# A masked softmax whose GpSimd set-up becomes the first turn of its load loop

## The chip, the cores and the metric

The kernel runs on one core of a Trainium2 chip. The metric is the time of one execution on the device in microseconds (us), as the median of several runs; lower is better. The core has four compute engines that matter here, each with its own stream of instructions: VectorE (DVE), ScalarE (ACT), GpSimd (POOL) and TensorE (PE). SyncE (SP) only issues transfers. Sixteen DMA engines move data between the device memory and the on-chip memory. Transfers issued by SP go through one queue, those issued by POOL through another, and both are served by the same sixteen engines. The profile calls SP's queue q1, POOL's queue q0, and the queue that brings the engines their code q14.

## The reference

For each of 16 batches, a softmax over the first `length` columns of each row, and zero behind them:

```python
def setup_inputs():
    batch, heads, seq_q, seq_k = 16, 8, 256, 256
    return {
        "x": np.random.randn(batch, heads, seq_q, seq_k).astype(np.float32),
        "lengths": np.random.randint(seq_k // 2, seq_k, size=batch).astype(np.int32),
    }

def reference(x, lengths):
    result = np.zeros_like(x)
    for b in range(batch):
        length = lengths[b]
        masked = x[b, :, :, :length].copy()
        masked = masked - np.max(masked, axis=-1, keepdims=True)
        exp_masked = np.exp(masked)
        result[b, :, :, :length] = exp_masked / np.sum(exp_masked, axis=-1, keepdims=True)
    return result.astype(np.float32)
```

The draw is the same each time. A batch is 2048 rows of 256 columns in float32, 2 MB.

## The kernel before

**Tiles.** A batch lies on chip as 128 partitions x 16 rows x 256 columns, in one of eight slots of the tile `xt`; batch b is in slot b % 8. The work is done in place: a slot is loaded, clipped, exponentiated, divided and stored.

**Loads.** SP loads batches 0 to 3 whole, without waiting (L128 to L132). POOL loads batches 4 to 15 in a loop of six turns (L177), two batches in a turn (`par` 0 and 1). Of these batches only as many columns are loaded as are needed: `pick` (L147) is a tree of compares of the batch's length with the widths 160, 168, ... 240, and each of its twelve leaves holds one transfer of a fixed width (256 in the last). The tree stands twice in the loop, once for each `par`. Before its tree, each `par` reads the length into a register (L120 called from L180) and, from the second turn on, waits until its own load before has landed (L182, `s_sw`) and until the store that frees the slot is done (L183, `s_st`).

**Set-up on POOL.** Ahead of the loop POOL makes `iota_i` (L164), `ones` and `ones_c` (L167, L168), two small writes that raise the store semaphores once so that the loop's counts fit (L170), waits for two steps of DVE (L171), clears the columns from 160 on in slots 4 to 7 with four memsets (L173), and waits for the lengths, for its own memsets and for the load of batch 2 (L174 to L176). Columns behind a narrow load must hold something finite; from the ninth batch on a slot holds old results there.

**DVE.** From `iota_i` it makes `down` (L204), a large negative ramp; from the lengths, spread to all partitions by a PE matmul with `ones` (L189), it makes `len_s` (L212). Per batch it clips x by the minimum with `down` + `len_s` (L221), so that columns behind the length become hugely negative and their exponential is zero. When ACT is done with half a batch, DVE takes the reciprocal of the sums (L245) and multiplies (L248).

**ACT.** A loop over the 32 halves of batches (L321) runs eight exponentials with row sums each (L326).

**Stores.** SP, in order of batches, in one to three parts (L136 to L143). It begins when the third half has been exponentiated (L134). From batch 2 on it waits at the first part until the store two batches earlier is done (L140).

**End.** DVE checks the extremes of the row sums (L274 on); only if they are out of range a slower version with the true maximum runs, which doesn't happen with this draw. SP waits for all stores (L355).

Of the kernel before, what the change touches and what calls it, by code (L numbers as in the profile page):

```python
# [17 lines left out]
POOL = mybir.EngineType.Pool  # L18
# [3 lines left out]
def kernel(  # L22
# [6 lines left out]
    nc = tc.nc  # L29
    P = nc.NUM_PARTITIONS  # L30

    batch, heads, seq_q, seq_k = x.shape
# [8 lines left out]

    slots = 8
    ahead = 4
    assert slots - ahead == 4 and batch % slots == 0

    widths = list(range(160, 248, 8))
    low = widths[0]
# [18 lines left out]
    xt = pool.tile([P, slots, nt, seq_k], F32, name="xt")  # L66
    word64 = pool.tile([1, batch], mybir.dt.int64, name="word64")
    word = word64.bitcast(I32)
    len_b = pool.tile([1, batch], BF16, name="len_b")
    ones = pool.tile([1, P], BF16, name="ones")  # L70
    len_f = psum.tile([P, batch], F32, name="len_f")
    len_s = pool.tile([P, batch], F32, name="len_s")
    iota_i = pool.tile([P, seq_k], I32, name="iota_i")
# [4 lines left out]
    seed = pool.tile([1, 2], F32, name="seed")  # L78

    sum_low, sum_high = 1.0e-15, 1.0e30  # L80
    ones_c = pool.tile([P, 1], BF16, name="ones_c")
# [10 lines left out]
    s_st = [sem("s_st0"), sem("s_st1")]  # L92
    with tc.tile_critical(no_gpsimd_drain=True):  # L93
        s_word = sem("s_word")
        s_ones = sem("s_ones")
        s_lenb = sem("s_lenb")
        s_lenf = sem("s_lenf")
        s_ld = [sem(f"s_ld{k}") for k in range(ahead + 1)]

        s_sw = [sem("s_sw0"), sem("s_sw1")]  # L100

        s_iota = sem("s_iota")
        s_fill = sem("s_fill")
        s_v = sem("s_v")
# [13 lines left out]
        def length(engine, at):  # L118

            return nc.values_load(  # L120
                at,
                engines=[engine],
                skip_runtime_bounds_check_because="compared with constants, never an address",
            )
# [22 lines left out]
        def pick(v, n, slot, par, ws):  # L147

            if len(ws) == 1:
                w = ws[0]  # L150
                nc.gpsimd.dma_start(  # L151
                    out=xt[:, slot, :, :w], in_=x_n[:, n, :, :w]
                ).then_inc(s_sw[par], 16)
                return
            m = (len(ws) - 1) // 2
            with nc.gpsimd.If(v <= ws[m]):  # L156
                pick(v, n, slot, par, ws[: m + 1])
            with nc.gpsimd.Else():
                pick(v, n, slot, par, ws[m + 1 :])
# [1 line left out]
        x_n = x_f.rearrange("b p t c -> p b t c")  # L161
        x_g = x_f.rearrange("b p t c -> p b (t c)")
        o_g = out_f.rearrange("b p t c -> p b (t c)")
        nc.gpsimd.iota(  # L164
            iota_i, pattern=[[1, seq_k]], base=0, channel_multiplier=0
        ).then_inc(s_iota, 1)
        nc.gpsimd.memset(ones, 1.0).then_inc(s_ones, 1)  # L167
        nc.gpsimd.memset(ones_c, 1.0).then_inc(s_ones, 1)  # L168
        for par in range(2):
            nc.gpsimd.memset(seed[:, par : par + 1], 0.0).then_inc(s_st[par], 64)  # L170
        nc.gpsimd.wait_ge(s_v, 2)  # L171
        for b in range(ahead, slots):
            nc.gpsimd.memset(xt[:, b, :, low:], 0.0).then_inc(s_fill, 1)  # L173
        nc.gpsimd.wait_ge(s_word, 16)  # L174
        nc.gpsimd.wait_ge(s_fill, slots - ahead)
        nc.gpsimd.wait_ge(s_ld[ahead - 1], 16)  # L176
        with nc.Fori(0, (batch - ahead) // 2, 1, engines=[POOL]) as q:  # L177
            for par in range(2):
                n = 2 * q + (ahead + par)
                v_len = length(POOL, word[0:1, bass.ds(2 * n, 1)])  # L180
                with nc.gpsimd.If(q >= 1):  # L181
                    nc.gpsimd.wait_ge(s_sw[par], 16 * q)  # L182
                    nc.gpsimd.wait_ge(s_st[par], 64 * q)  # L183
                pick(v_len, bass.ds(n, 1), bass.ds(n % slots, 1), par, widths + [seq_k])


        nc.tensor.wait_ge(s_ones, 2)
# [198 lines left out]
```

## Time and profile before

| what | value |
|---|---|
| time, median of 3 runs | 156.16 us (155.8 to 156.35) |
| time of the profiled execution | 156.34 us |
| span of that execution in the profile | 154.7 us |
| DVE busy | 116.6 us, 75% of the span |
| ACT busy | 105.2 us, 68% |
| POOL busy | 19.0 us, 12% |
| bytes moved by the DMA engines | 62.09 MB, mean 401 GB/s |
| share of q1 (SP), q0 (POOL) in 16 engines' span | 65.7%, 32.1% |
| POOL's 12 issues of loads (L151) | mean 1064 ns each |
| POOL's 4 clearing memsets (L173) | mean 1391 ns each |

The span runs from the first to the last instruction of the program; the time has what lies around it as well. The profile names a group of work by its line, engine and operation, then the tile that it writes and those that it reads ("xt<-in_x_dram" is a load of x into `xt`). An engine's name with a q (POOLq, SPq) stands for its sequencer: reading registers, branching, waiting, issuing. In the chain of waits, "issue" is time for which the profile shows no cause.

### The profile page before, as it was taken

What the parts mean: (1) busy time and instruction counts of PE and PEld (TensorE: products, weight loads), DVE (VectorE), ACT (ScalarE), POOL (GpSimd) and SP (SyncE); (2) the same over time, 40 slices, a digit from 0 to 9 for tenths busy, and PEclk for the clock granted to TensorE, in tenths of its full rate; (3) what the DMA queues carried; (4) which work ended last, traced back from release to release, by engine and by line L of the source; (5) the groups of instructions that cost most, each with busy time, mean ns of one, the idle gap of its engine ahead of it and who ended that gap; (6) DMA issues with size and microseconds to landing.
All of it is one profiled execution on the core that took longest, in us unless ns stands there. A gap on an engine that the chain in (4) does not pass through costs nothing.

```text
span 154.7 us, 1341 instructions
## 1 busy us (share of the span) xinstructions
PE 0.3 (0%) x2; PEld 0.2 (0%) x2; DVE 116.6 (75%) x89; ACT 105.2 (68%) x514; POOL 19.0 (12%) x26
## 2 busy tenths in 40 slices
PE   0000000000000000000000000000000000000000
PEld 0000000000000000000000000000000000000000
DVE  1349999953999696979879696969669619696820
ACT  3097799992692959688695959595964914959300
POOL 4910031000220200202020020202001000000000
DMA  3999999999999999999999999999999999999991
GB/s 114 430 447 419 441 373 420 403 407 447 406 403 391 410 410 417 412 416 412 404 422 409 415 412 409 421 414 412 415 424 415 416 437 432 422 447 424 424 426 76
DMA packets 9989, 62.09 MB, mean 401 GB/s; under 512 B 850, under 2 KB 946, under 8 KB 6274
## 3 DMA queue, kind: packets, MB, share of 16 engines
q1 hardware_dynamic: 5904, 41.95, 65.7%
q0 software_dynamic: 4080, 20.12, 32.1%
q14 instruction: 3, 0.02, 0.0%
q10 hardware_dynamic: 2, 0.00, 0.0%
HBM read 28.51 MB, written 33.55 MB: 401 GB/s over the span
## 4 chain that ended last, share of the span: by engine, by line
DMA 77%; issue 7%; DVE 4%; ACT 3%; POOLq 3%; SPq 1%; ACTq 0%; POOL 0%; PE 0%; DVEq 0%
DMA xt<-in_x_dram 77%; ACT xt L326 3%; DVE xt L221 2%; DVE xt L248 1%; POOLq L120 1%; POOLq L156 1%; POOLq L151 1%; SPq L130 1%; DVE ends L274 0%; ACTq L326 0%; POOL xt L151 0%; SPq L132 0%; POOLq L181 0%; DVE bad L277 0%; DVE inv_sum L245 0%
## 5 line engine op out<-in xcount | busy, mean ns | idle before, releaser
L326 ACT ACTIVATE xt<-xt x256 | 102.4, 402 | 37.7 <-DVE xt L221 37.7
L248 DVE TENSOR_TENSOR xt<-xt,inv_sum 128x2048 f32<-128x2048 f32 x32 | 73.3, 2291 | 1.1
L326 ACT ACTIVATION_READ_ACCUMULATOR xt<-xt x256 | 48.0, 188 | 0.0
L221 DVE SCALAR_TENSOR_TENSOR xt<-down,len_s,xt 128x2048 f32<-128x2048 f32 (+1 forms) x17 | 37.8, 2221 | 13.6 <-DMA xt<-in_x_dram 13.5
L151 POOL DMA_DIRECT2D xt<-in_x_dram x12 | 12.8, 1064 | 96.0 <-DMA out_dram<-xt 54.2
L245 DVE RECIPROCAL inv_sum<-row_sum 128x8 f32<-128x8 f32 x32 | 6.3, 198 | 14.4 <-ACT xt L326 14.4
L173 POOL MEMSET xt<- 128x1536 f32 x4 | 5.3, 1391 | 1.1 <-DVE len_s L212 1.1
L318 ACT ACT_TABLE_LOAD x1 | 1.3, 1283 | 1.6 <-SPq L93 1.6
L204 DVE TENSOR_SCALAR down<-iota_i 128x256 f32<-128x256 int32 x1 | 0.3, 301 | 1.6 <-POOL iota_i L164 1.6
L274 DVE TENSOR_REDUCE ends<-row_sum 128x1 f32<-128x256 f32 x2 | 0.7, 411 | 0.0
L191 PE MATMUL count<-bad,ones_c 128*1 128x2 bf16 x1 | 0.2, 164 | 145.3 <-DVE bad L277 145.3
L209 DVE CAST len_b<-word 1x16 bf16<-1x16 int32 x1 | 0.2, 164 | 0.4 <-DMA word<-in_lengths_dram 0.4
L212 DVE TENSOR_SCALAR len_s<-len_f 128x16 f32<-128x16 f32 x1 | 0.2, 173 | 0.3 <-PE len_f L189 0.3
L164 POOL IOTA iota_i<- 128x256 int32 x1 | 0.3, 331 | 0.6 <-SPq L93 0.6
L285 DVE TENSOR_REDUCE redo<-count 1x1 f32<-1x2 f32 x1 | 0.1, 148 | 0.3 <-PE count L191 0.3
L191 PEld LDWEIGHTS count<-bad,ones_c 128*1 128x1 bf16 x1 | 0.1, 79 | 145.4 <-DVE bad L277 145.4
L170 POOL MEMSET seed<- 1x1 f32 x2 | 0.2, 226 | 0.0
L277 DVE TENSOR_SCALAR bad<-ends 128x1 bf16<-128x1 f32 x2 | 0.2, 152 | 0.0
L318 ACT ACTIVATE warm<-const-float32-0.0 128x1 f32<-128x1 f32 x1 | 0.2, 204 | 0.0
L167 POOL MEMSET ones<- 1x128 bf16 x1 | 0.2, 196 | 0.0
L189 PE MATMUL len_f<-len_b,ones 1*128 1x16 bf16 x1 | 0.2, 165 | 2.6 <-DVE len_b L209 2.6
L370 POOL MEMSET const-float32-0.0<- 128x1 f32 x1 | 0.1, 98 | 0.3 <-issue 0.3
(6 smaller groups left out, 0.5 us busy)
## 6 DMA issues: line engine op xcount, KB each, us to landing
out_dram<-xt SPq DMA_DIRECT2D x19, 1024.0 KB
out_dram<-xt SPq DMA_DIRECT2D x14, 512.0 KB
xt<-in_x_dram SPq DMA_DIRECT2D x3, 2048.0 KB, 16.0
out_dram<-xt SPq DMA_DIRECT2D x3, 2048.0 KB
xt<-in_x_dram POOLq DMA_DIRECT2D x3, 1728.0 KB, 16.9
xt<-in_x_dram POOLq DMA_DIRECT2D x2, 2048.0 KB, 18.5
xt<-in_x_dram POOLq DMA_DIRECT2D x2, 1600.0 KB, 17.1
xt<-in_x_dram POOLq DMA_DIRECT2D x2, 1280.0 KB, 15.1
```

What stands on the lines that cost most here:

```text
L120: return nc.values_load(at, engines=[engine], skip_runtime_bounds_check_because="compared with constants, never an address",)
L130: nc.sync.dma_start(out=xt[:, 0, s], in_=x_f[0, :, s]).then_inc(s_ld[h], 16)
L151: nc.gpsimd.dma_start(out=xt[:, slot, :, :w], in_=x_n[:, n, :, :w]).then_inc(s_sw[par], 16)
L156: with nc.gpsimd.If(v <= ws[m]):
L173: nc.gpsimd.memset(xt[:, b, :, low:], 0.0).then_inc(s_fill, 1)
L191: nc.tensor.matmul(count, lhsT=ones_c, rhs=bad, start=True, stop=True).then_inc(s_count, 1)
L221: return nc.vector.scalar_tensor_tensor(out=t, in0=down[:, None, lo:hi].to_broadcast([P, s.stop - s.start, hi - lo]), scalar=len_s[:, b : ...
L245: step(nc.vector.reciprocal(out=inv_sum[:, b, s], in_=row_sum[:, b, s]))
L248: nc.vector.tensor_tensor(out=t, in0=t, in1=inv_sum[:, b, s, None].to_broadcast([P, half, seq_k]), op=ALU.mult,).then_inc(s_out, 1)
L274: step(nc.vector.tensor_reduce(out=ends[:, k : k + 1], in_=sums, op=op, axis=AX))
L318: nc.scalar.activation(out=warm, in_=nc.const_aps.tensor(0.0, (P, 1), F32), func=EXP)
L326: ins = nc.scalar.activation(out=e, in_=e, func=EXP, accum_out=sum_h[:, bass.ds(i, 1), j])
```

## The change

POOL's loop gets one more turn, seven instead of six. In the first turn (`turn` 0) it runs the set-up, unchanged and in the same order; in the others the body of the old loop. The two are the branches of one `If` on `turn >= 1`: the true branch holds the two trees of loads, the `Else` branch the set-up. So in the program's order the set-up's code comes behind the code of the loads. The old loop variable `q` is worked out of `turn` as (turn + 7) % 8, which is turn - 1 for turns 1 to 6. The condition for the waits, `q >= 1`, becomes `turn >= 2`. All waits, counts and transfers stay as they are.

```diff
@@ -41,7 +41,7 @@
-    assert slots - ahead == 4 and batch % slots == 0
+    assert slots - ahead == 4 and batch % slots == 0 and (batch - ahead) // 2 < 8
@@ -161,27 +161,34 @@
-        nc.gpsimd.iota(
-            iota_i, pattern=[[1, seq_k]], base=0, channel_multiplier=0
-        ).then_inc(s_iota, 1)
-        nc.gpsimd.memset(ones, 1.0).then_inc(s_ones, 1)
-        nc.gpsimd.memset(ones_c, 1.0).then_inc(s_ones, 1)
-        for par in range(2):
-            nc.gpsimd.memset(seed[:, par : par + 1], 0.0).then_inc(s_st[par], 64)
-        nc.gpsimd.wait_ge(s_v, 2)
-        for b in range(ahead, slots):
-            nc.gpsimd.memset(xt[:, b, :, low:], 0.0).then_inc(s_fill, 1)
-        nc.gpsimd.wait_ge(s_word, 16)
-        nc.gpsimd.wait_ge(s_fill, slots - ahead)
-        nc.gpsimd.wait_ge(s_ld[ahead - 1], 16)
-        with nc.Fori(0, (batch - ahead) // 2, 1, engines=[POOL]) as q:
-            for par in range(2):
-                n = 2 * q + (ahead + par)
-                v_len = length(POOL, word[0:1, bass.ds(2 * n, 1)])
-                with nc.gpsimd.If(q >= 1):
-                    nc.gpsimd.wait_ge(s_sw[par], 16 * q)
-                    nc.gpsimd.wait_ge(s_st[par], 64 * q)
-                pick(v_len, bass.ds(n, 1), bass.ds(n % slots, 1), par, widths + [seq_k])
+
+        turns = (batch - ahead) // 2
+        with nc.Fori(0, turns + 1, 1, engines=[POOL]) as turn:
+            with nc.gpsimd.If(turn >= 1):
+                q = nc.s_assert_within(
+                    (turn + 7) % 8, 0, turns - 1, skip_runtime_bounds_check_because="turn >= 1"
+                )
+                for par in range(2):
+                    n = 2 * q + (ahead + par)
+                    v_len = length(POOL, word[0:1, bass.ds(2 * n, 1)])
+                    with nc.gpsimd.If(turn >= 2):
+                        nc.gpsimd.wait_ge(s_sw[par], 16 * q)
+                        nc.gpsimd.wait_ge(s_st[par], 64 * q)
+                    pick(v_len, bass.ds(n, 1), bass.ds(n % slots, 1), par, widths + [seq_k])
+            with nc.gpsimd.Else():
+                nc.gpsimd.iota(
+                    iota_i, pattern=[[1, seq_k]], base=0, channel_multiplier=0
+                ).then_inc(s_iota, 1)
+                nc.gpsimd.memset(ones, 1.0).then_inc(s_ones, 1)
+                nc.gpsimd.memset(ones_c, 1.0).then_inc(s_ones, 1)
+                for par in range(2):
+                    nc.gpsimd.memset(seed[:, par : par + 1], 0.0).then_inc(s_st[par], 64)
+                nc.gpsimd.wait_ge(s_v, 2)
+                for b in range(ahead, slots):
+                    nc.gpsimd.memset(xt[:, b, :, low:], 0.0).then_inc(s_fill, 1)
+                nc.gpsimd.wait_ge(s_word, 16)
+                nc.gpsimd.wait_ge(s_fill, slots - ahead)
+                nc.gpsimd.wait_ge(s_ld[ahead - 1], 16)
```

## The prediction, made before the changed kernel was run

> **What bounds the kernel now.** I read the page's slices first, then the queues, the chain of waits, and last the windows at the two ends.
>
> ```profile
> DMA  3999999999999999999999999999999999999991
> HBM read 28.51 MB, written 33.55 MB: 401 GB/s over the span
> DMA 77%; issue 7%; DVE 4%; ACT 3%; POOLq 3%; SPq 1%; ACTq 0%; POOL 0%; PE 0%; DVEq 0%
> ```
>
> The 16 DMA engines are full from the second slice to the last. No engine comes near that (DVE 75%, ACT 68% of the span), and 77% of the chain is loads of x in flight. So the bound is the moving of 62.09 MB. A change that moves no byte can gain only if the bytes move faster, or if data are put in the queues earlier at an end of the span; it can lose only what the stores standing in the queue can't fill.
>
> Next, GpSimd (POOL) in order of time, since the change touches it alone, and the chain of waits around its first load:
>
> ```profile
> 1.24 0.33 POOL L164 IOTA iota_i<- 128x256 int32 x1 [0.62 <-SPq L93]
> 3.05 5.33 POOL L173 MEMSET xt<- 128x1536 f32 x4 [1.10 <-DVE len_s L212]
> 20.77 1.29 POOL L151 DMA_DIRECT2D xt<-in_x_dram  x1 [12.39 <-issue]
> 23.96 0.56 POOL L151 DMA_DIRECT2D xt<-in_x_dram  x1 [1.90 <-issue]
> ```
>
> ```profile
> 18.54 0.04 POOLq L176
> 18.59 0.05 issue
> 18.64 0.03 POOLq L177
> 18.66 0.03 issue
> 18.70 0.09 POOLq L177
> 18.79 0.03 issue
> 18.82 0.51 POOLq L120
> 19.32 0.03 issue
> 19.35 0.04 POOLq L181
> 19.40 0.12 issue
> ```
>
> Each row is start, duration, who. Set-up is over at 8.4 us; POOL then waits for the load of batch 2, which lands at 18.52, and needs 2.2 us more (register read L120, compares, address work) until it issues the load of batch 4 at 20.77. The load of batch 5 follows at 23.96. From there on a POOL load is issued about 1.4 us after the load two batches earlier has landed (43.37 to 44.81, for example), so the twelve loads are two chains of six, and what is late in the first turn stays late in the chain.
>
> The last 4 us:
>
> ```profile
> 147.14 0.37 SPq L141 DMA_DIRECT2D out_dram<-xt  x1
> 150.00:151.00 1.00, 0.00 (x0) 0.00 (x0) 0.00 (x0) 0.00 (x0) 0.00 (x0) 1.00 1.04 442
> 151.00:152.00 1.00, 0.00 (x0) 0.00 (x0) 0.00 (x0) 0.00 (x0) 0.00 (x0) 1.00 0.47 197
> 152.00:153.00 1.00, 0.00 (x0) 0.00 (x0) 0.00 (x0) 0.00 (x0) 0.00 (x0) 1.00 0.10 41
> ```
>
> The last two columns of a window are the DMA share and GB/s. The final store (1024 KB) is issued at 147.14, but the engines are still full of earlier stores past 150, and a few of them run on to about 153. SP's first load is issued at 1.13 and the loads begin to move at about 2.5, so 1.4 us from issue to first packet. The final store could thus have begun at 148.5; at 427 GB/s it takes 2.5 us. On the engines that finish last, near 152.9, it begins at 150.4. **Spare at the end: 150.4 - 148.5 = 1.9 us** (an estimate from these rows). Those engines set the end, not the last computation.
>
> **The change, part by part.** No transfer, tile, wait value or semaphore count changes, and SP, ACT, DVE and PE keep their instructions and order. What differs is where POOL's code stands and which branches it takes.
>
> *Set-up starts behind a branch.* Ahead of IOTA come the loop's register move (0.06 us from its start to the next row, 18.64 to 18.70), perhaps one register operation (0.09), and one taken compare-branch (L181: 0.04 plus 0.12 to the next). Together 0.2 to 0.3 us; I take 0.3. The cover: DVE sits idle 0.39 us for the lengths after making `down`, and its first clip waits 3.53 us for x although `len_s` is ready. So up to some 3.9 us of lateness here reach nobody on DVE. POOL's four clearing memsets end at 8.4 and are needed at 18.5; ten us. Cost 0. With the cover gone it would be 0.3.
>
> *The loop is entered by its back edge.* After the last wait (L176, 18.54) the old code ran a move (0.06); the new code runs the loop's add and jumps back. In the old first turn's end that took from 23.94 (add) to 24.3 (the loop's first register operation): +0.34. Then a new compare, turn >= 1: 0.07 if it falls through (L156: 0.04 plus 0.03), 0.16 if taken. Then the remainder arithmetic for q: nothing if it is fused with the operations that stand there (0.08 to 0.09 now), at most another 0.15. Sum: -0.06 + 0.34 + 0.07 to 0.16 + 0 to 0.15 = 0.35 to 0.59. I take **0.45 us later for the load of batch 4**, and the same for batch 5 behind it.
>
> *Later turns.* Extra compare, arithmetic and the jump over the set-up (about 0.4 by the same rows) stand ahead of L182's waits, and POOL sits there for 4 us or more each time (the second turn waits until its load lands at 37.3). Cost 0.
>
> *What is queued behind the late load.* DVE waits 4.39 us for batch 4 (until 37.51) and gets it 0.45 later, then ACT, then SP's store. The DMA engines don't wait. The queue view has no POOL-queue packet between 20 and 26 us although the load was issued at 20.77: in that time SP's queue moves the load of batch 3 and then the store of batch 0. The stores of batch 1 and 2 follow, and between 36 and 42 us they still take a fifth of the engines' time. So stores move into the gap, the total stays, and the lateness appears at the last load (landing 134.2). There the spare of 1.9 takes it. I let a third of it through (0.15), since the spare is an estimate and a mix of reads and writes that is shifted moves at other rates (400 to 430 GB/s in the slices).
>
> *Code loading.* This is the unknown part: the trace of before jumps forward nowhere so far.
>
> ```profile
> q14 instruction: 3, 0.02, 0.0%
> ```
>
> Three packets of code in the whole span. By windows of the queue view, none lies in the first 25 us, one in 25 to 26, one in 60 to 61, one after 134. Up to 24.0 POOL ran through both trees and the back edge, so all pages it touched there were in place before the span. The set-up now lands where the loop's end stood, about as many instructions in. Hence I take 0 for both jumps. The bounds: below, a packet is moved out of the busy time, -0.3 (1.9% of 16 engines' us in window 25 to 26); above, the jump back at 18.6 finds the loop's top gone and loads it through full engines. For that no row exists; from below 0.3 (the packet), from above 5.2 (POOL's own load, 20.77 until after 26). I'd take 2.5 if it happens.
>
> [...]
>
> **Sum.** The profiled execution took 156.34 with a span of 154.7; its end moves by +0.15, to 156.5. It lies 0.18 above the median of the three runs, 156.16, so for the median: **156.3 us**.
>
> **Rivals.**
> 1. *Faster, 155.5.* In the window 21.00 to 22.50 the rate is 317 GB/s beside some 430 around it: (430 - 317) x 1.5 / 430 = 0.39 us lost, just while POOL issues its first load (20.77, 1.29 us). If the later issue meets the end of batch 3's load elsewhere, that goes; with a code packet of 0.3 that moves to the idle start, 0.69 is gained. For: the coincidence in time. Against: no other POOL issue has such a dip beside it, and the packet counts only on an engine that ends last.
> 2. *Slower, 157.2: the jump back stalls for code.* At 18.6, price 0.45 + 2.5 = 2.95 us, of which the spare of 1.9 hides the first part: +1.05. It decides from a stall of 1.45 on (1.9 - 0.45); at 5.2 it is +3.75. For: set-up and loop top now lie some hundred instructions apart, and the jump falls in full DMA. Against: the code packets above.
> 3. *The lateness isn't absorbed, 156.7.* The chains of loads carry 0.45 to 0.59 to the last landing, and the spare doesn't hold because it was read on a few late engines alone: +0.45 to +0.6.
> If set-up were not placed behind the trees, the branches would cost the same and this is the forecast again.
>
> **How the numbers follow.** Forecast (absorbed) 0.38, rival 1 0.25, rival 2 0.19, rival 3 0.18. About 0.3%, 0.47 us, is what a measurement of this kernel tells from no change. Forecast: 0.31 within, 0.03 faster, 0.04 slower. Rival 1: 0.22 faster, 0.03 within. Rival 2: slower. Rival 3: 0.06 within, 0.12 slower. Faster 0.25, within 0.40, slower 0.35. The forecast's own range is 155.9 to 156.7. The whole reaches from a little below rival 1 (155.3) to the middle of rival 2 (157.6), which leaves out some 0.06 below and 0.12 above.
>
> **What would show it.** Right: IOTA at 1.4 to 1.6; POOL's first load at 21.1 to 21.4, and the last landing up to 0.6 later; DMA share unbroken; final store by 147.6. IOTA past 3 us shows a stall at the first jump, harmless until 3.9. A code packet between 18 and 25 us with the first load after 22.5 shows rival 2. A rate of 400 or more in 21 to 22.5 shows rival 1. The prediction is wrong if the DMA engines show a gap, or if the time moves over 0.5 us with POOL's loads in place.

## The result and the profile after

| | before | after |
|---|---|---|
| time, median of 12 runs each | 156.19 us (155.8 to 156.5) | 156.62 us (156.01 to 157.24) |
| profiled execution | 156.34 us | 156.98 us |
| its span | 154.7 us | 155.4 us |
| POOL's set-up begins (IOTA) | 1.24 us | 1.84 us |
| load of batch 2 has landed | 18.52 us | 19.07 us |
| POOL's first load is issued | 20.77 us | 22.00 us |
| last load has landed | 134.18 us | 133.86 us |
| final store is issued | 147.14 us | 146.85 us |
| last two DMA engines are done with it | 152.62, 153.02 us | 152.97, 153.80 us |

The changed kernel takes 1.0032 of the time before, with a 95% interval of 1.0019 to 1.0045: slower by 0.3%, some 0.5 us. In the experiments below, three single executions (159.44 and 159.64 us of after_wait_inside, 159.48 us of before_half) lie over 1.5% above the fastest of their kernel and are left out of its ratio. The page after, in the lines that answer to those shown of before (slices, bytes, code packets):

```profile
DMA  4999999999999999999999999999999999999990
HBM read 28.51 MB, written 33.55 MB: 399 GB/s over the span
q14 instruction: 3, 0.02, 0.0%
```

The same bytes and the same three packets of code; the DMA engines are full throughout. Next, POOL in order of time:

```profile
1.84 0.33 POOL L179 IOTA iota_i<- 128x256 int32 x1 [1.22 <-SPq L93]
3.16 5.34 POOL L188 MEMSET xt<- 128x1536 f32 x4 [0.61 <-DVE len_s L219]
22.00 1.30 POOL L151 DMA_DIRECT2D xt<-in_x_dram  x1 [13.50 <-issue]
24.74 0.56 POOL L151 DMA_DIRECT2D xt<-in_x_dram  x1 [1.45 <-issue]
```

IOTA is 0.6 us late, but the four clearing memsets only 0.1. The first load is 1.23 us late. The chain of waits (start, duration, who) says where that comes from:

```profile
2.51 16.57 DMA xt<-in_x_dram
19.07 0.02 issue
19.10 0.04 POOLq L191
19.14 0.05 issue
19.19 0.04 POOLq L178
19.23 0.12 issue
19.34 0.05 POOLq L166
19.39 0.03 issue
19.42 0.04 POOLq L166
19.47 0.21 issue
19.68 0.03 POOLq L166
19.71 0.03 issue
19.73 0.04 POOLq L167
```

From the end of the wait (L191) to the issue it is now 2.90 us instead of 2.23: +0.67, for a branch out of the set-up (L178), the loop's add and back edge (L166) and the new compare (L167). The other 0.55 stand in the first line: in before the load of batch 2 landed after 16.01 us, here after 16.57. POOL has no hand in that load.

The queue view of the changed kernel for the microsecond from 4 to 5 (packets, MB, share of 16 engines) shows what is new there:

```profile
q1 hardware_dynamic: 52, 0.43, 102.0%
q14 instruction: 1, 0.01, 2.0%
```

Of the three packets of code, the one that came at 25.4 us now comes at 4.6, 3.4 us after POOL's jump to the set-up (at 1.22) and in the middle of the first load. It takes 0.315 us on its DMA engine, and the data packet that starts behind it took 0.51 instead of 0.31. So one engine is some 0.5 us behind, and the load of batch 2 has landed when the last engine is done: POOL goes on at 19.10, behind the sixteenth landing at 19.07 and not behind the fifteenth at 18.48. The sixteenth landings show it, beside the fifteenth, in both kernels:

```
landed, us (15th / 16th engine)   before          after
first half of batch 0             6.23 / 6.26     6.18 / 6.81
batch 2                          18.51 / 18.52   18.48 / 19.07
batch 3                          23.74 / 23.79   23.37 / 24.66
batch 5                          43.16 / 43.37   43.53 / 44.89
batch 6                          51.67 / 51.88   52.74 / 52.79
batch 9                          78.81 / 79.19   79.73 / 79.78
batch 15 (the last load)        133.89 / 134.18 133.79 / 133.86
```

In the first loads fifteen engines are as early as before, and one is alone behind. It is the one that carried the code packet: in the packet records of the changed kernel up to 25 us, nine packets in ten start 3 or 4 ns before the end of the one ahead of them, so this engine can be followed that far. One engine stays alone behind up to batch 5. At batch 6 the last two engines are within 0.05 us of each other, and at the last load within 0.07. So the traces don't show one engine that stays behind for the whole kernel.

At the end of the span, in the windows of the changed kernel (last columns: DMA share, GB/s) and in SP's waits (total, times, longest):

```profile
150.00:151.00 1.00, 0.00 (x0) 0.00 (x0) 0.00 (x0) 0.00 (x0) 0.00 (x0) 1.00 0.99 418
151.00:152.00 1.00, 0.00 (x0) 0.00 (x0) 0.00 (x0) 0.00 (x0) 0.00 (x0) 1.00 0.64 270
152.00:153.00 1.00, 0.00 (x0) 0.00 (x0) 0.00 (x0) 0.00 (x0) 0.00 (x0) 1.00 0.18 74
153.00:154.00 1.00, 0.00 (x0) 0.00 (x0) 0.00 (x0) 0.00 (x0) 0.00 (x0) 1.00 0.04 16
```

```profile
SPq L388 <- DMA out_dram<-xt: 4.3, 1, 4.3
```

A share of 0.04 in the last window is less than one engine of sixteen (0.06): a single engine works until 153.8, after a final store that was issued 0.29 us earlier than in before. SP waits 4.3 us for it instead of 3.4. So in this execution the loss isn't in the computation. Which engine this is, the landings don't say.

### The profile page after: what moved, and what is told of

It reads as the page before. It is cut to its first block, busy times and chain, and to the rows that moved or that the text cites. A ratio compares the mean times of both kernels' runs of the same rounds, so it can differ in the third digit from the quotient of the medians.

```text
span 155.4 us, 1364 instructions
## 1 busy us (share of the span) xinstructions
PE 0.3 (0%) x2; PEld 0.2 (0%) x2; DVE 116.6 (75%) x89; ACT 105.2 (68%) x514; POOL 19.0 (12%) x26
## 4 chain that ended last, share of the span: by engine, by line
DMA 76%; issue 7%; DVE 4%; ACT 3%; POOLq 3%; SPq 1%; ACTq 0%; POOL 0%; PE 0%; DVEq 0%
DMA xt<-in_x_dram 76%; ACT xt L333 3%; DVE xt L228 2%; DVE xt L255 1%; POOLq L120 1%; POOLq L156 1%; POOLq L151 1%; SPq L130 1%; DVE ends L281 0%; ACTq L333 0%; SPq L132 0%; POOLq L174 0%; POOL xt L151 0%; DVE bad L284 0%; DVE inv_sum L252 0%
## 6 DMA issues: line engine op xcount, KB each, us to landing
xt<-in_x_dram POOLq DMA_DIRECT2D x3, 1728.0 KB, 16.4
```

## The experiments

Three theories. **A**: the code packet that the jump to the set-up brings early holds up one DMA engine, every transfer waits for that engine, and it ends last. **B**: POOL's first load is 1.2 us late, and that reaches the end. **C**: the late start of the set-up and the longer way into the loop cost the time. The sum of what they gave (ratios to before, with 95% intervals; times in us from one profiled execution of each; "done" is when the last two engines have finished the final store):

```
                     POOL code  batch 2 landed  first load  last load  final   last two       ratio
                     packet at   15th / 16th    by POOL     landed     store   done
before                25.4      18.51 / 18.52   20.77       134.18     147.14  152.62 153.02
after (12 runs)        4.6      18.48 / 19.07   22.00       133.86     146.85  152.97 153.80  1.0032 (1.0019-1.0045)
after_again            4.7      18.52 / 19.17   22.09       134.12     147.05  152.63 153.42  1.0054 (1.0037-1.0071)
setup_first           22.6      18.48 / 18.50   24.84       134.90     147.90  152.43 152.85  1.0018 (1.0000-1.0036)
late_only             26.3      18.50 / 18.64   22.17       133.03     146.02  152.69 152.69  0.9997 (0.9984-1.0010)
after_wait_inside      4.6      18.38 / 19.12   20.55       135.47     148.37  152.79 152.84  1.0036 (1.0015-1.0057)
before_half           27.0      18.44 / 18.59   20.84       135.58     148.58  153.43 153.55  1.0069 (1.0051-1.0086)
after_half             4.4      18.46 / 18.91   21.82       137.53     150.51  154.56 154.62  1.0146 (1.0121-1.0170)
early_packet       4.5, 26.0    18.42 / 18.95   21.25       133.22     146.16  152.88 153.53  1.0067 (1.0048-1.0086)
late_setup            25.5      18.58 / 18.62   20.87       134.08     147.05  152.58 153.02  1.0003 (0.9991-1.0014)
before_wait_inside    24.4      18.44 / 18.52   19.93       133.89     146.88  152.49 153.02  1.0003 (0.9991-1.0016)
one_engine_16k        26.0      18.54 / 19.21   21.47       133.57     146.56  152.96 153.25  1.0022 (1.0000-1.0044)
one_engine            29.4      19.42 / 23.42   25.92       140.85     153.77  157.83 157.87  1.0245 (1.0222-1.0268)
```

**after_again.** The changed kernel once more, beside the next three.

> The changed kernel once more, on the chip on which the other experiments of this group run. Ratio to before 1.002 to 1.0045. In the trace the code packet lies between 4 and 6 us, the load of batch 2 lands about 0.5 us later than in before (18.5), and POOL's first load is issued at about 22.0. Theory A (the early code packet holds up one DMA engine, which then ends last) expects one engine behind the other fifteen by 0.5 us or more from the first load's landing to the final store's landing. Theory B (POOL's first load is 1.2 us late, and the lateness reaches the end) expects the last load and the final store to be late as well.

The loss is there again, 1.0054, somewhat above the expected range, and so is the one late engine. The last load and the final store are within 0.1 us of before. That speaks for A and against B. Its profiled execution is the fastest of its six (156.59 us) and shows only a part of the loss.

**setup_first.** The same loop and compares, with the code in the old order.

```diff
-            with nc.gpsimd.If(turn >= 1):
-                ... loads ...
-            with nc.gpsimd.Else():
-                ... set-up ...
+            with nc.gpsimd.If(turn < 1):
+                ... set-up ...
+            with nc.gpsimd.Else():
+                ... loads ...
```

> The set-up is still the first turn of the loop, with all its compares and the back edge, but its code stands ahead of the code of the loads again (the branch is on turn < 1, the loads are in the Else). Theory A: no code packet before 18 us, the load of batch 2 lands at 18.5 again, POOL's first load is issued at about 21.4, and the time is that of before within 0.15% (ratio 0.9985 to 1.0015). Theory B: half of the lateness is left (0.65 of 1.23 us), ratio about 1.0015 to 1.003.

No early packet, no late engine, and batch 2 landed at 18.50 again; but the first load came at 24.84, not 21.4. Its chain of waits shows a stall ahead of that issue, where before has 0.65 us:

```profile
21.10 0.04 POOLq L151
21.14 3.67 issue
24.81 0.02 POOLq L158
```

3.0 us more, with the code packet at 22.6 in the middle, which points to a wait of POOL for code. Although its first load was 4.07 us late, the ratio is 1.0018, with an interval that begins at 1.0000. So this kernel lies just outside A's range, being late for a reason of its own. The 1.0018 is inside B's range, but that was for a lateness of 0.65 us; more than three times the changed kernel's 1.23 us doesn't cost more here, which speaks against B. At the last load only 0.72 of the 4.07 us are left.

**late_only.** Before, with POOL's first load held back.

```diff
         nc.gpsimd.wait_ge(s_ld[ahead - 1], 16)
+        nc.gpsimd.memset(pad, 0.0).then_inc(s_pad, 1)
+        nc.gpsimd.wait_ge(s_pad, 1)
```

> The kernel before with one more memset on POOL (1344 columns of a tile that nobody reads) and a wait for it between the last wait of the set-up and the loop: POOL's first load is issued about 1.25 us later, and nothing else is changed. Theory A: the DMA queues fill the gap with stores, ratio 0.9985 to 1.0015, the last load's landing within 0.5 us of before. Theory B: ratio 1.002 to 1.0045, as the changed kernel.

In order of time:

```profile
18.78 1.22 POOL L179 MEMSET pad<- 128x1344 f32 x1 [10.39 <-DMA xt<-in_x_dram]
22.17 1.29 POOL L153 DMA_DIRECT2D xt<-in_x_dram  x1 [2.18 <-issue]
```

The first load is 1.4 us late, later than in the changed kernel, and the time is 0.9997. The last load even landed 1.15 us earlier, more than the 0.5 us that A allowed. B falls: the lateness is absorbed.

**after_wait_inside.** The changed kernel with an earlier first load.

```diff
                     with nc.gpsimd.If(turn >= 2):
                         nc.gpsimd.wait_ge(s_sw[par], 16 * q)
                         nc.gpsimd.wait_ge(s_st[par], 64 * q)
+                    with nc.gpsimd.Else():
+                        nc.gpsimd.wait_ge(s_ld[ahead - 1], 16)
...
-                nc.gpsimd.wait_ge(s_ld[ahead - 1], 16)
```

> The changed kernel with the wait for the load of batch 2 moved from the end of the set-up to the place behind the reading of the length in the first turn of loads (an Else to the waits of the later turns): the back edge, the compare and the register read then lie ahead of the wait, and POOL's first load is issued about 1.4 us after the landing, 20.4 to 20.6, which is earlier than in before. The early code packet stays. Theory A: the loss stays, ratio 1.002 to 1.0045. Theory B: the loss is gone or turned into a gain, ratio 0.997 to 1.0005.

POOL's first load is earlier than in before (20.55), the early packet stays, and so does the loss. In the profiled execution, one of the fastest of its twelve, the engines end nearly together and the last load is late instead.

**before_half and after_half.** Both kernels with seven leaves to a tree (`widths = list(range(160, 248, 16))`).

> The kernel before with widths of 160 to 240 in steps of 16 instead of 8, so each tree has seven leaves instead of twelve and POOL's code in the loop is some 50 instructions shorter; some narrow loads become 8 columns wider, so more bytes are read. It is the base for after_half. No code packet for POOL before 18 us, and perhaps none at all. Both theories: ratio 1.000 to 1.010, for the bytes.

> The changed kernel with the same seven widths. The set-up's code now stands behind some 50 instructions less. If the packet of code comes when POOL first runs an instruction far enough from its start, the jump to the set-up no longer brings one at 4 to 6 us. Theory A (the early packet is the cause) then expects before_half's time within 0.15%, and the load of batch 2 at 18.5. A theory C (it is the set-up's later start and the longer way into the loop, or the longer loop) expects the loss to stay: 0.2 to 0.6% above before_half. If the packet still comes early, A expects the loss to stay too.

This pair was to move the packet by shorter code, and failed in that: the packet still comes at 4.4. The loss stays, as A expects of that case, at 158.22 to 157.12 us by the medians (0.7%). C expects it too, so the pair tells nothing between them. The traces show another way for the loss to reach the end, that of late loads: against before_half the last load is 1.95 us late, the final store 1.93, and the engines end together at 154.6, within 0.2 us of each other, waiting for that store.

**early_packet.** Before, with a jump at the start and nothing else of the change.

```diff
+        with nc.Fori(0, 2, 1, engines=[POOL]) as z:
+            with nc.gpsimd.If(z >= 1):
+                for k in range(112):
+                    nc.gpsimd.memset(pad[:, k : k + 1], 0.0).then_inc(s_pad, 1)
+            with nc.gpsimd.Else():
+                ... set-up up to its memsets ...
+        nc.gpsimd.wait_ge(s_pad, 112)
```

> The kernel before with a loop of two turns around the set-up: the second turn holds 112 tiny memsets, whose code stands ahead of the set-up's, and runs after it, while POOL has nothing to do (8 to 16 us). So POOL jumps far ahead at the start as in the changed kernel, but the loop of loads is entered as in before and isn't longer. Theory A: a code packet at 4 to 6 us, one engine 0.5 us behind at the landing of the first loads, the load of batch 2 at about 19.0, ratio 1.002 to 1.006. Theory C: ratio 0.9985 to 1.0015, since only the start of the set-up is late.

The queue view from 4 to 5 us:

```profile
q14 instruction: 1, 0.01, 2.0%
```

The packet is there, one engine is 0.5 us behind, and the kernel takes 1.0067, although the loop of loads is entered as in before and the last load landed earlier. The loss is just above the expected range. Here the packet comes on top of the one at 26.0, which stays; that may be why it costs more than in the changed kernel. What the 112 small memsets (8.45 to 12.20 us, while POOL only waits) cost by themselves wasn't tested.

**late_setup.** Before, with one memset of 640 columns ahead of IOTA.

> The kernel before with one memset of 640 columns of an unread tile ahead of everything on POOL, so that the set-up begins 0.6 us late (IOTA at about 1.85, as in the changed kernel) and nothing jumps. The code packet stays at 25 to 27 us. Theory A: ratio 0.9985 to 1.0015. Theory C: part of the loss comes with the late set-up, ratio 1.002 or more.

1.0003. The 0.6 us by which the set-up begins later cost nothing, and C loses its first half. Its other half, the longer way into the loop, is lateness of the first load, which late_only has shown to be free. The longer loop of the later turns wasn't tested by itself; setup_first has the same loop, so 1.0018 (1.0000 to 1.0036) bounds its cost.

**one_engine and one_engine_16k.** Before, with the hold-up made by data instead of code.

```diff
+        nc.scalar.dma_start(out=pad, in_=x_g[:31, 0, :1024]).then_inc(s_pad, 16)
```

(The smaller one takes `:128`.)

> The kernel before with one more transfer at the start, from ACT's queue: 31 rows of 4 KB (127 KB) of x into a tile that nobody reads, of a shape that I expect to be given to one DMA engine alone, which is then 4 to 5 us behind the others; a wait for it at the end. Theory A: what holds up one engine at the start is not made up, since each transfer is shared out evenly: the landings of the first loads are 4 to 5 us later, one engine ends that much behind the rest, and as at most 1.9 us of that is hidden the ratio is 1.012 to 1.03. Theory B or C: the lateness of the loads alone costs little, ratio below 1.006. If the transfer is spread over all engines it costs 0.3 us and tells nothing.

> As one_engine, with 31 rows of 512 bytes (16 KB) instead of 127 KB: one engine is held up by about 0.6 to 1.0 us at the start, near what the code packet costs its engine in the changed kernel (0.5). Which engine it is isn't chosen. Theory A: if it is one of those that end last anyway, ratio 1.002 to 1.006; if it is one of the many that end 1 to 1.5 us before the last, ratio 0.9985 to 1.002. The load of batch 2 lands 0.3 to 1.0 us late in any case. Theory C: 0.9985 to 1.0015.

The chain of waits of the large one begins like this, with batch 2 landing at 23.42:

```profile
2.51 20.91 DMA xt<-in_x_dram
```

One engine is 4.0 us behind the fifteenth, and the kernel loses 2.45%, 3.8 us of the 4.9 that it is late in landing batch 2. The expectation that this engine ends 4 to 5 us behind the rest was wrong: it is 2.0 us behind at batch 5 and 0.3 at the last load, and all engines end within 0.2 us of each other. The time goes where the other engines run out of work: early, while the loads wait for the late engine, and near the end, where the last load has landed 6.7 us late. Three windows of this kernel, and the third of them in before (last columns: DMA share, GB/s):

```profile
22.00:24.00 2.00, 0.00 (x0) 0.00 (x0) 0.35 (x1) 2.00 (x11) 0.00 (x0) 1.00 0.57 236
30.00:32.00 2.00, 0.00 (x0) 0.00 (x0) 2.00 (x2) 2.00 (x11) 0.00 (x0) 1.00 0.78 237
144.00:148.00 4.00, 0.00 (x0) 0.00 (x0) 2.84 (x3) 3.31 (x17) 0.00 (x0) 1.00 0.36 152
```

```profile
144.00:148.00 4.00, 0.00 (x0) 0.00 (x0) 3.35 (x6) 0.55 (x4) 0.00 (x0) 1.00 0.96 408
```

(The profiled execution, 161.28 us, is the slowest of its five.) The small one lags by 0.67 us, near the changed kernel's 0.59, and costs 1.0022, with an interval that begins at 1.0000. No code packet comes early in either. So a held-up engine alone costs time: the large one shows it, the small one is at the edge of what can be told. That it is the whole of the changed kernel's loss isn't shown.

**before_wait_inside.** The wait behind the reading of the length, in the kernel before.

> The kernel before with the wait for the load of batch 2 behind the first reading of a length, so that POOL's first load is issued at 19.9 to 20.1 instead of 20.8. If an earlier first load were worth what a later one would cost under theory B, ratio 0.996 to 0.999. Theory A: no code packet is moved, ratio 0.9985 to 1.0015.

The first load is issued 0.84 us earlier, and the ratio is 1.0003. An early first load is worth as little as a late one costs. None of these versions beats the kernel before.

## Why the prediction was right or wrong

**Right: the time is near that of before.** 156.3 was said and 156.62 measured, in the likeliest case's own range, at the edge of what was called no change; the sign of the small rest is clear of zero. Part of that is luck: three of the forecast's own signs were missed. IOTA came at 1.84 (said: 1.4 to 1.6), POOL's first load at 22.00 (21.1 to 21.4), and the last landing was 0.32 earlier (up to 0.6 later).

**Right, but not by the way described: the lateness of POOL's first load is absorbed.** The prediction let what is late in the first turn stay late in the chain, appear at the last load, and be hidden by the spare at the end. Instead the lateness melts on the way. Against before, batch 5 landed 1.5 us later, batch 7 1.0, batch 9 0.6, batch 11 0.4, and batches 13 and 15 0.3 earlier: a load that is issued later took less time to land (batch 7 16.4 us instead of 16.9, batch 9 15.7 instead of 16.2). The part about the stores fits: they fill the gap (DMA stays at 9 in every slice of the page but the first and the last). The spare, put at 1.9 us, was sized well, though this lateness never came to it. In after_half and one_engine, where all engines end within 0.2 us of each other, 4.1 us go by from the final store's issue to the last engine's end (150.51 to 154.62, 153.77 to 157.87). In before it is 147.14 to 153.02, 5.9 us: a spare of 1.8. Rival 3 falls with late_only.

**Mis-sized: the way into the loop.** 0.35 to 0.59 us were worked out, 0.67 measured. The branch that leaves the set-up (L178, 0.15 us to the next row) wasn't counted.

**Mis-sized, without effect: the set-up's start.** 0.3 us were taken, 0.6 measured: the jump took 0.52 us from the compare to the next row, where a taken branch took 0.16. The cover of 3.9 us was there, as late_setup shows.

**Wrong: code loading at no cost.** This is the step that failed. I concluded from the absence of packets before 25 us that all code was in place and both jumps free. For the two jumps that was nearly right. What was missed is that the jump to the far code moves a packet: the one of 25.4 came at 4.6. In early_packet, after and setup_first a code packet follows a far jump (0.46 to 0.52 us from the compare to the next row) by 3.2, 3.4 and 4.0 us; what ties the two isn't shown. I had priced a moved packet as a gain of 0.3, on the thought that it leaves the busy time. It went from one busy place to another, 2.4 us into the first load, where it put one engine 0.5 us behind, and the load of batch 2 was complete only with that engine (19.07 us, the fifteenth at 18.48).

**Right for a wrong reason: the 0.15 let through.** I let it through from the late load. The experiments put the loss on the one engine that is held up.

**Rival 1 (faster).** The window that it rested on did change, but the dip only moved. In the changed kernel:

```profile
21.00:22.50 1.50, 0.00 (x0) 0.00 (x0) 1.47 (x3) 1.50 (x9) 0.50 (x1) 1.00 1.03 426
26.00:28.00 2.00, 0.00 (x0) 0.00 (x0) 2.00 (x2) 2.00 (x11) 0.00 (x0) 1.00 0.90 319
```

426 GB/s instead of 317 in the first, and 319 instead of 379 in the second. It wasn't POOL's issue that slowed the engines: in after_wait_inside the issue is at 20.55, and the dip is late as well (393 in the first window, 347 in the second). It moves with the engine that is behind: in one_engine_16k, where POOL's code is that of before, the two are 448 and 325.

**Rival 2 (a stall for code in busy time).** It doesn't happen in the changed kernel: from the back edge's compare to the next row it takes 0.25 us, as in before. A stall of that kind shows in setup_first: 3.0 us more ahead of the first load, near the 2.5 that were estimated, with the packet at 22.6 in it; and there it costs 0.3 us by the ratio, as most of the lateness has melted by the last load. The 0.36 us extra at the changed kernel's first jump aren't such a wait: POOL goes on at 1.75, and the first packet comes at 4.6. What the packet did show in the changed kernel is a hold-up of the data on the engine that carries it (0.51 us for the data packet behind it instead of 0.31).

**What stays open.** How the hold-up of one engine reaches the end isn't shown. Landings carry no engine's name, and the lone engine of the first loads is no longer alone from batch 6 on, so that it is the one that ends last is not shown. The gap between the last two engines at the end is 0.83, 0.79 and 0.65 us in after, after_again and early_packet, but 0.05 and 0.06 in after_wait_inside and after_half, which have the early packet too and lose by a late last load; in the kernels without it and without a held-up engine it is up to 0.53 (before_wait_inside). Between 19 and 25 us the engine falls back from 0.6 to 1.3 us: by the packet records it takes 1.13 and 0.92 us for two packets of 16 KB, from 21.68 on, that take 0.61 otherwise. In before seventeen packets of 16 KB are slow (0.76 us or more) between 20.9 and 22.5, in the changed kernel two there and thirteen between 25.8 and 27.3; the cause isn't known. Nor is it shown whether a packet at 25 us costs less than one at 4.6, and why, nor which code the packet holds.

## What to carry to other kernels

In this kernel the DMA engines set the time, and a load was there when the last of its sixteen parts had landed (batch 2 at 19.07 us, fifteen parts by 18.48). So a small thing on one engine could cost most of its size (3.8 us for the 4.0 by which the transfer of 127 KB put one engine behind), while 1.4 us of lateness in issuing was free (late_only, 0.9997). Before moving code in a kernel like this, look where the code packets lie in the queue view, and ask not only whether a jump stalls (3.0 us in setup_first) but when a packet of code will come behind it (3.2 to 4.0 us in three kernels here) and what it will stand in front of. To find such an engine, compare the sixteenth landing of the first load with the fifteenth.

## What the hardware showed unexpectedly

- A packet of 8 KB of code held up its engine by 0.5 us amid a load, and one engine was alone behind, by 0.6 to 1.4 us, in the landings up to 44.9 us.
- A transfer of 31 rows went to one engine alone: it has one closing packet of 4 bytes, where each load has sixteen. For 127 KB that engine was 4.0 us behind at batch 2 (23.42 us, the fifteenth at 19.42), and the kernel lost 3.8 us.
- The engines have a dip in rate that comes later when one engine is some 0.6 us behind: from 21 to 22.5 us 317 GB/s in before, but 426 in the changed kernel, 393 in after_wait_inside and 448 in one_engine_16k. From 26 to 28 us the kernels with such an engine have 311 to 347, those without 344 to 424; one_engine, whose engine is 4.0 us behind, has 393 there.
- POOL's first load may be issued between 19.9 and 22.2 us without a measurable difference (1.0003, 0.9997).
